# Three gaps before the tile pools of an MLP: the place of the added weight tiles modulo 256 bytes

## The chip, the cores and the metric

The kernel runs on one core of one Trainium2 chip. The metric is the device time of one execution in microseconds (us), the median of several runs. The core has five engines that run side by side, each with its own stream of instructions: TensorE (PE in the profile; PEld is its loading of weights), VectorE (DVE), ScalarE (ACT), GpSimd (POOL) and SyncE (SP, which here only issues transfers). They work on an on-chip memory of 128 partitions; a tile is a stretch of bytes at the same address in every partition. "Place modulo 256" below means that byte address modulo 256.

## The reference

One layer of an encoder, in float32, for 256 tokens of width 2048: a mixer with four groups of channels (gated linear attention, a Fourier transform, two long convolutions with learned filters, a short convolution), a cross attention to 256 memory rows, and an MLP, each with an RMS norm before it and a residual sum behind it. The change concerns the MLP alone:

```python
def swiglu(h, w_gate_up, w_down):
    gate, up = jnp.split(h @ w_gate_up, 2, axis=-1)
    return (jax.nn.silu(gate) * up) @ w_down
...
x = x + swiglu(rms_norm(x, norm_g[l, 2]), w_gate_up[l], w_down[l])
```

`w_gate_up` is 2048 x 11264 and `w_down` is 5632 x 2048.

## The kernel before

All weights come as a stream of slabs. A slab (`raw`, 128 x 2048 float32, 1 MB) holds 16 blocks of 128 x 128, in the order in which TensorE uses them. SyncE issues the transfers (`Stream.raw`, line 102) into the three buffers of pool `rawp`; during the gate/up product every fourth slab goes into one more buffer, `rawx`.

Products are made in float32r, with each float32 number split into a high and a low part: `Stream.split` casts a half slab of 1024 columns into `wh` on ScalarE (line 120) and subtracts this from the original into `wl` on VectorE (line 121). A product then takes three matmuls (`Block.part`, lines 449, 450 and 451): high by high, high by low, low by high. In the MLP the activations are the stationary operand and 512 columns of `wh` or `wl` are the moving one.

The pairs of tiles `wh` and `wl` come from pools: `wp` has three pairs, for the whole kernel; `wp2` has two more, for the gate/up product alone. `Stream.free` gives a half slab to the first of the two pools that has a pair free. A tile has 1088 columns, of which 1024 are used, starting at column `at`:

```python
at = 48 if any(a <= n < b for a, b in ROWS) else 8
...
wh, wl = (pool.tile([P, 1088], F32R, name=t, tag=t) for t in ("wh", "wl"))
wh, wl = wh[:, at:at + 1024], wl[:, at:at + 1024]
```

In the MLP `at` is 48, which is 192 bytes. The tiles of `wp` begin at 192 modulo 256, so the operand begins at 128. The tiles of `wp2` begin at 128, so there the operand begins at 64.

The MLP (`mlp`, line 853) opens pool `fp`, then `wp2`, `rawx`, `sw` (sums of activations, split) and `gp` (`u`, `m`, `g`, `h`), and calls `gate_up`; when this is done it closes them and opens `hp`, with the `held` tiles and the later `f` tiles, and calls `down`. Pools are laid out one behind the other, so a tile that is put into one pool moves all that are opened after it. `gap` (line 295) allocates such a tile and does nothing with it. The tiles with activations (`act`, `f`, the formed sums) begin at 128.

`gate_up` runs over 11 groups of 512 gate and 512 up columns, and in each over 8 pairs of 128-row steps of the contraction. Some of the pairs (two in groups 1 to 3, three in groups 4 to 10) are computed with seven products of halves in place of eight; for these VectorE also forms differences and sums of weight blocks in place in the slab (line 150). `combine` and `finish` then add the parts, apply silu and the product, turn the result (line 478) and send it to memory through GpSimd's queue (`hidden`, line 481); `fetch` brings it back (line 879). `down` (line 1025) runs over 4 groups of 512 output columns with 44 steps each; the operands of its last half slabs are the `held` tiles.

The order of the instructions is written out by the program; small pieces of other work (`Background`) are put between the matmuls at fixed points, by a count of work and not by measured time.

Of the kernel before, what the change touches and what calls it, by code (L numbers as in the profile page):

```python
# [246 lines left out]
class Block:  # L247
# [605 lines left out]
    def mlp(self):  # L853
        tc, nc, act, st = self.tc, self.nc, self.act, self.st
        with tc.tile_pool(name="fp", bufs=1) as fp:
            self.gap(fp, 192)
            f = act[4:12] + [fp.tile([P, 512], F32R, name=f"f{i}") for i in range(EARLY - 8)]
            with tc.tile_pool(name="wp2", bufs=2) as wp2, tc.tile_pool(name="rawx", bufs=1) as st.rawx, \
                    tc.tile_pool(name="sw", bufs=1) as sw, tc.tile_pool(name="gp", bufs=1) as gp:
                st.pools.append([wp2, 2])  # L860
                self.gate_up(sw, gp, f)
            st.pools.pop()
            st.rawx = None
            with tc.tile_pool(name="hp", bufs=1) as hp:
                held = [hp.tile([P, 512], F32R, name=f"held{i}") for i in range(HELD // 2)]
                self.st.places = list(zip(held[0::2], held[1::2]))
                f += [hp.tile([P, 512], F32R, name=f"g{i}") for i in range(FT - 16 - EARLY)] + self.h3
                self.bg.add(self.fetch(f, EARLY, FT, 6, SOON))
                self.down(f)
# [806 lines left out]
```

## Time and profile before

| | |
|---|---|
| median of 3 runs | 1472.63 us (1472.04 to 1472.85) |
| the profiled execution | 1474.72 us |
| its span, from the first instruction to the last | 1472.9 us |
| TensorE busy | 1458.6 us (99%) |
| VectorE busy | 1105.7 us (75%) |
| ScalarE busy | 815.1 us (55%) |
| bytes read from memory | 291.18 MB |
| mean granted clock of TensorE | 0.996 |

The page of a profile gives the busy time of each engine, its share in 40 slices of the span, the clock that TensorE was granted, and the chain of work that ended last. Views of the trace give more: windows (the busy time of each engine and the count of its instructions in a stretch of time), the timeline (instructions in order of time, with start and duration), and waits (who waited for whom). Times in views are from the start of the span. A matmul's duration in the trace is longer than the distance to the next one, because matmuls are pipelined and their ends are modelled; the distance between starts tells the pace.

### The profile page before, as it was taken

To read this page: it belongs to the slowest core of one execution; us is meant where nothing else is said; L and a number is where in the kernel's file an instruction comes from. 1 tells how busy PE (TensorE), PEld (TensorE's weight loads), DVE (VectorE), ACT (ScalarE), POOL (GpSimd) and SP (SyncE) were. 2 spreads that over 40 slices of the span, in tenths; PEclk is the share of its full clock that TensorE was granted. 3 is DMA by queue.
4 is the path that set the end of the run, shared out by engine and by line. 5 is a ranking of instruction groups with operands and counts; after the bars stand their busy time and mean duration, and the time that the engine had idled before them with its cause. 6 is when DMAs were issued, how large, how long until landed. Compare 5 with 4: busy or idle time off the path is not lost.

```text
span 1472.9 us, 19616 instructions
## 1 busy us (share of the span) xinstructions
PE 1458.6 (99%) x7275; PEld 1229.1 (83%) x7275; DVE 1105.7 (75%) x1608; ACT 815.1 (55%) x1209; POOL 161.7 (11%) x276
## 2 busy tenths in 40 slices
PE   9999999999999999999999999999999999999997
PEld 8878888898898888888888888888888888888886
DVE  6588768778767767877786888999999996644445
ACT  6556655467555546765564555555555554534344
POOL 0220100000000001100015322221101113000000
PEclk9999999999999999999999999999999999999999
DMA  9985554454535556544556865666666655655554
GB/s 351 350 262 201 204 200 172 146 182 160 208 129 204 184 180 223 180 172 174 200 203 211 273 235 205 217 218 224 223 218 241 217 196 187 243 185 192 198 198 145
DMA packets 56720, 306.11 MB, mean 208 GB/s; under 512 B 9485, under 2 KB 11182, under 8 KB 25008
## 3 DMA queue, kind: packets, MB, share of 16 engines
q1 hardware_dynamic: 45920, 281.11, 53.9%
q0 software_dynamic: 10272, 23.09, 5.3%
q8 instruction: 57, 0.93, 0.3%
q10 hardware_dynamic: 432, 0.66, 0.1%
q14 instruction: 39, 0.32, 0.1%
HBM read 291.18 MB, written 13.63 MB: 207 GB/s over the span
## 4 chain that ended last, share of the span: by engine, by line
PE 97%; DVE 1%; ACT 1%; DMA 0%; issue 0%; SPq 0%; ACTq 0%
PE pg L398 18%; PE pg L450 15%; PE pg L451 15%; PE pg L449 15%; PE pg L399 10%; PE pm L450 6%; PE pm L451 6%; PE pm L449 6%; PE pm L1177 1%; PE pg L395 1%; PE pg L396 1%; PE pm L846 1%; PE pm L819 0%; DVE wl L121 0%; DMA raw<-in_W 0%; PE pm L1557 0%
## 5 line engine op out<-in xcount | busy, mean ns | idle before, releaser
L121 DVE TENSOR_TENSOR wl<-raw,wh 128x1024 fp32r<-128x1024 f32 (+2 forms) x557 | 657.2, 1190 | 283.5 <-ACT wh L120 277.0
L120 ACT CAST wh<-raw 128x1024 fp32r<-128x1024 f32 (+2 forms) x557 | 566.3, 1023 | 521.8 <-PE pg L451 230.7
L398 PE MATMUL pg<-act,wh 128*128 128x512 f32 x1104 | 390.3, 395 | 2.9 <-DVE act L276 2.9
L399 PE MATMUL pg<-act,wl 128*128 128x256 f32 x1216 | 341.8, 281 | 0.0
L450 PE MATMUL pg<-wl,act 128*128 128x512 f32 (+1 forms) x779 | 304.1, 390 | 1.8 <-DVE wl L121 1.8
L449 PE MATMUL pg<-wh,act 128*128 128x512 f32 (+1 forms) x779 | 304.5, 392 | 0.0
L451 PE MATMUL pg<-wh,act 128*128 128x512 f32 (+1 forms) x779 | 303.9, 390 | 0.0
L398 PEld LDWEIGHTS pg<-act,wh 128*128 128x128 f32 x1104 | 208.7, 189 | 48.7 <-DVE act L276 3.3
L399 PEld LDWEIGHTS pg<-act,wl 128*128 128x128 f32 x1216 | 229.8, 189 | 0.8 <-DVE wl L121 0.5
L450 PEld LDWEIGHTS pg<-wl,act 128*128 128x128 f32 x779 | 146.4, 188 | 33.8 <-DVE wl L121 2.7
L449 PEld LDWEIGHTS pg<-wh,act 128*128 128x128 f32 x779 | 146.5, 188 | 32.5 <-issue 0.8
L451 PEld LDWEIGHTS pg<-wh,act 128*128 128x128 f32 x779 | 146.4, 188 | 31.8 <-issue 0.4
L450 PE MATMUL pm<-wl,act 128*128 128x512 f32 x288 | 112.7, 391 | 0.0
L449 PE MATMUL pm<-wh,act 128*128 128x512 f32 x288 | 112.6, 391 | 0.0
L451 PE MATMUL pm<-wh,act 128*128 128x512 f32 x288 | 112.6, 391 | 0.0
L481 POOL DMA_DIRECT2D hidden<-u x88 | 56.8, 654 | 306.0 <-DVE u L478 303.9
L150 DVE TENSOR_TENSOR raw<-raw 128x512 f32<-128x512 f32 (+1 forms) x81 | 70.2, 867 | 2.1
L449 PEld LDWEIGHTS pm<-wh,act 128*128 128x128 f32 x288 | 54.0, 187 | 12.2
L450 PEld LDWEIGHTS pm<-wl,act 128*128 128x128 f32 x288 | 54.0, 187 | 12.0
L451 PEld LDWEIGHTS pm<-wh,act 128*128 128x128 f32 x288 | 54.0, 187 | 12.0
L1014 POOL DMA_DIRECT2D xrows<-tmp x48 | 27.7, 585 | 137.6 <-DVE rc L280 126.6
L276 DVE TENSOR_TENSOR tmp<-pg,tmp 128x256 f32<-128x256 f32 x78 | 32.4, 417 | 5.4 <-ACT tmp L405 4.6
(343 smaller groups left out, 1652.0 us busy)
## 6 DMA issues: line engine op xcount, KB each, us to landing
raw<-in_W SPq DMA_DIRECT2D x246, 1024.0 KB, 5.0
raw<-in_W SPq DMA_DIRECT2D x11, 512.0 KB, 7.3
hidden<-u POOLq DMA_DIRECT2D x88, 64.0 KB, 4.7
tmp<-hidden POOLq DMA_DIRECT2D x44, 128.0 KB, 4.8
res<-in_xT SPq DMA_DIRECT2D x8, 512.0 KB, 8.3
k<-in_mem SPq DMA_DIRECT2D x8, 256.0 KB, 6.7
k<-in_x SPq DMA_DIRECT2D x8, 256.0 KB, 8.3
keys<-k POOLq DMA_DIRECT2D x32, 64.0 KB, 5.0
```

The costliest lines, as they stand in the source:

```text
L120: nc.scalar.copy(wh[:, a:b], r[:, a:b])
L121: nc.vector.tensor_tensor(out=wl[:, a:b], in0=r[:, a:b], in1=wh[:, a:b].bitcast(F32), op=ALU.subtract)
L150: op = lambda out, a, b, what=ALU.subtract: nc.vector.tensor_tensor(out=out, in0=a, in1=b, op=what)
L276: self.nc.vector.tensor_tensor(out=out, in0=a, in1=b, op=op)
L395: self.nc.tensor.matmul(p[:, 0:R], wh, slot[:, 0:R], start=start, stop=False)
L398: self.nc.tensor.matmul(p[:, :], wh, slot[:, :], start=start, stop=False)
L399: self.nc.tensor.matmul(p[:, 0:R], wl, slot[:, 0:R], start=False, stop=stop)
L449: self.nc.tensor.matmul(p, hi, wh, start=start, stop=False)
L450: self.nc.tensor.matmul(p, hi, wl, start=False, stop=False)
L451: self.nc.tensor.matmul(p, lo, wh, start=False, stop=stop)
L481: nc.gpsimd.dma_start(to[:, :, 32 * a:32 * a + 32], u[32 * a:32 * a + 32, :].rearrange("f (b t) -> f b t", t=32))
L1014: nc.gpsimd.dma_start(to[:, :, c:c + 32], u[32 * a:32 * a + 32, :].rearrange("t (b f) -> t b f", f=32))
```

## The change

Three gaps are added in `mlp`.

```diff
             self.gap(fp, 192)
             f = act[4:12] + [fp.tile([P, 512], F32R, name=f"f{i}") for i in range(EARLY - 8)]
+            self.gap(fp, 64)
             with tc.tile_pool(name="wp2", bufs=2) as wp2, tc.tile_pool(name="rawx", bufs=1) as st.rawx, \
                     tc.tile_pool(name="sw", bufs=1) as sw, tc.tile_pool(name="gp", bufs=1) as gp:
+                self.gap(sw, 192)
                 st.pools.append([wp2, 2])
                 self.gate_up(sw, gp, f)
             st.pools.pop()
             st.rawx = None
             with tc.tile_pool(name="hp", bufs=1) as hp:
+                self.gap(hp, 192)
                 held = [hp.tile([P, 512], F32R, name=f"held{i}") for i in range(HELD // 2)]
```

The first one moves `wp2` and `rawx` up by 64 bytes: the tiles of `wp2` and the buffer `rawx` go from 128 to 192 modulo 256. The second and the third one make the shift 256 bytes for what lies behind them (`sw` and `gp` in the gate/up product, `held` and the later `f` tiles in the down product), whose place modulo 256 stays. No instruction is added, removed or put elsewhere.

## Prediction

> **What bounds the kernel now.** I read the page first, for the engine that fills the span and for the granted clock.
>
> ```profile
> span 1472.9 us, 19616 instructions
> PE 1458.6 (99%) x7275; PEld 1229.1 (83%) x7275; DVE 1105.7 (75%) x1608; ACT 815.1 (55%) x1209; POOL 161.7 (11%) x276
> ...
> PEclk9999999999999999999999999999999999999999
> ...
> PE 97%; DVE 1%; ACT 1%; DMA 0%; issue 0%; SPq 0%; ACTq 0%
> ```
>
> TensorE is busy 99% of the span and is 97% of the chain that ended last, at full clock. A time that is saved between two matmuls is therefore saved at the end, as long as nothing else becomes late. So the question is only how far apart the matmuls start in the stage that the change touches, the gate/up product, and whether that distance can be set by where their operand lies.
>
> Busy time does not tell this (a matmul's row shows 0.39 us, and they overlap). I take windows from the start of one matmul to the start of a later one. A window's count is one more than the matmuls that start in it, because the one before still runs. The first table has the gate/up product and the down product.
>
> ```profile
> core 0: us, PE busy (x) PEld busy (x) DVE busy (x) ACT busy (x) POOL busy (x), PEclk, DMA share, GB/s
> ...
> 765.68:1224.52 458.84, 458.84 (x1998) 374.25 (x1997) 405.34 (x478) 250.04 (x281) 97.77 (x161) 1.00 0.65 224
> 1225.62:1456.61 230.99, 230.99 (x1020) 191.25 (x1019) 123.66 (x139) 102.14 (x130) 14.38 (x25) 1.00 0.57 199
> ```
>
> (The first matmuls of the gate/up product, before 765.68, are left out; they read pool wp.) In the down product 1019 matmuls take 230.99 us: 226.68 ns each. In the gate/up product 1997 matmuls of the same shape (128x128 stationary, 512 moving columns, float32r) take 458.84 us: 229.76 ns each. TensorE is never idle in either and the clock is 1.00 in both, so the gate/up product spends 1997 x 226.68 = 452.68 us at the down product's pace and **6.2 us on something else**. That is the whole prize, whatever causes it.
>
> To see which matmuls lose it, I followed the half slabs in the order of the program, with the address that each tile has. Moving operands in the three pairs of pool wp start at 192 + 4 x 48 bytes, that is at 128 modulo 256; those in the two pairs of wp2 start at 128 + 192, that is at 64. The next rows are the starts at which wp2 blocks begin and end (900.40 to 906.00 is two half slabs of wp2, then come three of wp), and the same stretches as windows.
>
> ```profile
> 900.40 0.39 PE L449 MATMUL pm<-wh,act 128*128 128x512 f32 x1
> ...
> 906.00 0.39 PE L449 MATMUL pm<-wh,act 128*128 128x512 f32 x1
> ...
> 908.74 0.39 PE L449 MATMUL pm<-wh,act 128*128 128x512 f32 x1
> ...
> 914.18 0.39 PE L449 MATMUL pg<-wh,act 128*128 128x512 f32 x1
> ```
>
> ```profile
> core 0: us, PE busy (x), PEclk, DMA share, GB/s
> 900.40:906.00 5.60, 5.60 (x25) 1.00 1.01 381
> 906.00:908.74 2.74, 2.74 (x13) 1.00 0.70 295
> 908.74:914.18 5.44, 5.44 (x25) 1.00 0.34 104
> 972.08:977.68 5.60, 5.60 (x25) 1.00 0.00 0
> 1001.82:1008.64 6.82, 6.82 (x31) 1.00 0.94 358
> 1451.17:1456.61 5.44, 5.44 (x25) 1.00 0.00 0
> ```
>
> From wp2, 24 matmuls take 5.60 us: 233.3 ns each. From wp, 24 take 5.44 us: 226.7 ns each. The difference, 6.67 ns, does not come from transfers: the wp2 window at 972 has a DMA share of 0.00 and the same 5.60 us, and the wp window at 1001.82 has a share of 0.94 and takes 6.82 us for 30 matmuls (227.3 ns). Nor does it come from the region of memory: the window at 1451 reads its moving operand from the held tiles, which lie at bytes 168,064 and up, where wp2 lay before, but start at 128 modulo 256, and its 24 matmuls take 5.44 us. The first window after a wp2 block is a little slow (2.74 us for 12, where 12 x 226.7 = 2.72): about 20 ns of catching up follow each block.
>
> **The change, part by part.** Instructions, their order and their waits stay the same on every engine and queue; only start addresses move. So there is nothing to add or remove, and each step is a change of duration.
>
> Gap of 64 bytes in fp. It moves wp2 and rawx up by 64 bytes. The moving operands in wp2 then start at 192 + 192 = 384, that is 128 modulo 256, like those in wp. Of the 1997 matmuls 792 take their moving operand from wp2 (two of the five pairs, so about two fifths; counted by the tiles' addresses). 792 x 6.67 ns = 5.28 us. The catching up goes too: there are 46 changes from wp2 back to wp, 46 x 20 ns = 0.92 us. Sum 6.2 us, which is the 6.2 us that the stage loses as a whole, worked out above without the addresses. All of it lies on the path, as TensorE has no idle time there.
>
> The buffer rawx moves from 128 to 192 modulo 256, where the three of rawp already are. No row groups transfers by address, so I bound it: the rows of waits below name no wait of TensorE, and none of ScalarE for a landing of raw, in the whole stage. Below, nothing: a transfer that lands earlier feeds no one earlier. Above, nothing until it eats the time by which the operands are ahead. I take zero.
>
> ```profile
> ACT wh L120 <- PE pg L451: 78.3, 64, 2.2
> ACT wh L120 <- PE pm L451: 68.6, 57, 2.2
> ACT wh L120 <- DVE raw L150: 41.9, 28, 2.4
> DVE wl L121 <- ACT wh L120: 41.5, 45, 1.8
> ```
>
> These rows (total us, times, longest) are of the stage from 766 to 1224 us. ScalarE's casts into wh wait 146.9 us for TensorE to give a tile back, so the makers of operands are ahead and held up by the reader.
>
> Gaps of 192 bytes in sw and hp. With the 64 they make 256, so the formed sums, u, m, g, h, the held tiles and the later f tiles keep their place modulo 256. Price zero both ways, by the held window (5.44 us) that already has this place.
>
> The casts and subtractions. They write wl and wh at 128 in wp and at 64 in wp2 today. VectorE does not fill the stage (405.34 of 458.84 us), so a change of some ns in either is hidden; the cover is that idle 53.5 us. But it is thinner in places, and a faster TensorE eats into it. The tightest operand that I found is the second half slab of the group that starts at 981.1 us:
>
> ```profile
> 980.49 1.18 DVE L121 TENSOR_TENSOR wl<-raw,wh 128x1024 fp32r<-128x1024 f32 x1
> ...
> 982.74 0.39 PE L450 MATMUL pm<-wl,act 128*128 128x512 f32 x1
> ...
> 1140.00:1160.00 20.00, 20.00 (x89) 16.40 (x88) 19.63 (x24) 11.33 (x13) 5.14 (x8) 1.00 0.51 155
> ```
>
> It is ready at 981.67 and used at 982.74, 1.07 us ahead. Near 1150 VectorE is busy 19.63 of 20 us, so in such a stretch it cannot follow a faster TensorE. But in each group of columns (11 groups in 459 us, some 42 us each) it also reaches the point where it waits for tiles, so what TensorE gains adds up over one group at most: 6.2 / 11 = 0.56 us. That is less than 1.07. The next thing to be late is this add, with 0.5 us left.
>
> By the sum the profiled execution, 1474.72 us with a span of 1472.9, would take 1468.5. The median of the three runs is 2.1 us below the profiled one; from it, 1472.63 - 6.2 = **1466.4 us**, 0.42% less.
>
> The Trainium skill, page "SBUF — State Buffer", section "Specifications (TRN2)", gives memory lines of 16 bytes and full bandwidth where each line is hit at least twice. Both 64 and 128 are multiples of 16 and the operand is contiguous, so by that page alone the start would not matter and the time would stay 1472.6. The windows above do not agree that nothing else matters (233.3 against 226.7 ns).
>
> **The rivals.**
> No change: what sets 233.3 ns is not the start modulo 256 but something else that goes with wp2, such as the order in which its tiles are used. For it: the rows cannot vary one without the other inside the pool. Against it: the held window, in the same region, and four different places of wp2 with one pace. Time 1472.6. The page named above would give the same.
>
> Gain given back: the adds become late and TensorE waits. For it: 19.63 of 20 us. Against: 0.56 us against 1.07. If each group lost half of its gain, 3.1 us would remain: 1469.5.
>
> Slower: all five pairs then share one place modulo 256, and a tile that is being written collides with the one that is read, so that all 1997 matmuls run at 233.3 ns. It decides if the quick pace of wp needs that its neighbours lie elsewhere. Price: 1997 x 6.67 = 13.3 us in place of 6.2, so 1472.6 + 7.1 = 1479.7. Against it: in the down product only the three wp pairs are in use, all at one place, written and read at once, at 226.68 ns.
>
> **How the numbers follow.** The forecast gets 0.88, no change 0.05, the gain half given back 0.04, slower 0.03. The runs of before spread over 0.8 us, and without the catching up the gain is 5.3 us (1467.3); so 1465.4 to 1468.2 holds about 8 in 10. No more than 6.2 us can be had, as none of the windows has a pace under 226.7 ns; the lower end is noise alone. 0.2% is 2.9 us, about what a measurement can tell from no change. Faster by more: the forecast and most of the half gain, 0.91; within: 0.06; slower: 0.03.
>
> **What the changed profile would show.** The window from the first to the last matmul of the gate/up product should fall from 458.84 to 452.7 us for the same count; two half slabs of wp2 should take 5.44 us. The down product's 230.99 us for 1019 should stay. Against the forecast would be a window that stays at 5.60 us for wp2, a wp window above 5.44, or idle time of TensorE before L450 with VectorE's L121 as what ended it. A granted clock under 1.00 in the stage would make it wrong in another way.

## The result, and the profile after

The changed kernel takes 1467.55 us (median of 6 runs, 1465.87 to 1469.45) against 1473.21 us before (median of 6, 1472.04 to 1477.14). The ratio is 0.9958 with a 95% interval of 0.9948 to 0.9968, so 4.7 to 7.7 us less; by the ratio itself 6.2 us, while the two medians differ by 5.7. The page of the changed kernel has nearly the same shares as that of before:

```profile
span 1467.7 us, 19616 instructions
PE 1452.5 (99%) x7275; PEld 1229.2 (84%) x7275; DVE 1105.3 (75%) x1608; ACT 814.5 (55%) x1209; POOL 161.4 (11%) x276
...
PE 97%; DVE 1%; ACT 1%; DMA 0%; issue 0%; SPq 0%; ACTq 0%
```

TensorE is still what bounds the kernel, VectorE and ScalarE work as long as before, and only PE's busy time fell, by 6.1 us. The windows from the start of the first undisturbed matmul of the gate/up product to its end, and over the down product up to its last matmul, say where (columns as in the prediction):

```profile
core 0: us, PE busy (x) PEld busy (x) DVE busy (x) ACT busy (x) POOL busy (x), PEclk, DMA share, GB/s
766.59:1219.26 452.67, 452.67 (x1998) 374.89 (x1997) 404.97 (x478) 249.42 (x281) 97.65 (x161) 1.00 0.66 227
1220.36:1459.08 238.72, 238.72 (x1054) 197.70 (x1053) 125.50 (x145) 105.73 (x136) 14.35 (x25) 1.00 0.57 197
```

The gate/up product takes 452.67 us for the 1997 matmuls that took 458.84, so 226.67 ns each. The down product has 1053 in 238.72 us, 226.70 ns, as before. Three windows show that nothing is left to tell the pools apart; the first and the last are two half slabs of wp2 (24 matmuls), the middle one three of wp (36), which follow a wp2 block:

```profile
core 0: us, PE busy (x), PEclk, DMA share, GB/s
836.42:841.86 5.44, 5.44 (x26) 1.00 0.99 384
841.86:850.02 8.16, 8.16 (x38) 1.00 0.27 111
794.26:799.70 5.44, 5.44 (x26) 1.00 0.98 328
```

(Where a window's edge is rounded down, one more matmul is counted, 26 in place of 25.) wp2 went from 5.60 to 5.44 us, and after it 36 matmuls of wp take 8.16 us, 226.7 ns each: the catching up is gone.

The profiled execution's span fell by 5.2 us and not by 6.2, as its gate/up product begins 0.9 us later than in the execution of before (766.59 against 765.68). That lies ahead of everything that the change touches, and it is spread: in the profiles below that leave the stage before as it is, the same point lies between 762.7 and 766.3 us. The MLP itself hardly varies: its gate/up product takes 452.66 or 452.67 us here, in wp2_only and in both64.

### The profile page after: what moved, and what is told of

It is laid out like the page before. It is cut to its first block, busy times and chain, and to the rows that moved or that the text cites. A ratio compares the mean times of both kernels' runs of the same rounds, so it can differ in the third digit from the quotient of the medians.

```text
span 1467.7 us, 19616 instructions
## 1 busy us (share of the span) xinstructions
PE 1452.5 (99%) x7275; PEld 1229.2 (84%) x7275; DVE 1105.3 (75%) x1608; ACT 814.5 (55%) x1209; POOL 161.4 (11%) x276
## 4 chain that ended last, share of the span: by engine, by line
PE 97%; DVE 1%; ACT 1%; DMA 0%; issue 0%; SPq 0%; ACTq 0%
PE pg L398 18%; PE pg L450 15%; PE pg L451 15%; PE pg L449 15%; PE pg L399 10%; PE pm L449 6%; PE pm L451 6%; PE pm L450 6%; PE pm L1180 1%; PE pg L395 1%; PE pg L396 1%; PE pm L846 1%; PE pm L819 1%; DVE wl L121 0%; DMA raw<-in_W 0%; PE pm L1560 0%
```

## The experiments

All medians below are beside runs of the kernel before on the same chip. Its median there was 1473.83 to 1474.16 us where an interval is given, so kernels are compared by their ratios: 0.9958 is the changed kernel.

**Which of the two moved pools it is.** The first kernel moves wp2 alone, the second rawx alone; what lies behind keeps its place.

```diff
 wp2_only: the first gap stays (fp, 64), and the second one goes into rawx
-                self.gap(sw, 192)
+                self.gap(st.rawx, 192)
```

```diff
 rawx_only
-            self.gap(fp, 64)
...
+                self.gap(st.rawx, 64)
                 self.gap(sw, 192)
...
-                self.gap(hp, 192)
+                self.gap(hp, 256)
```

> Only the wp2 tiles move (128 to 192 modulo 256); rawx stays at 128, everything behind keeps its place. Place theory (the start of the moving operand modulo 256 sets the pace): as the full change, 6.2 us under before, the gate/up stretch near 452.7 us, two half slabs of wp2 in 5.44 us. Rival (the place of rawx does it): as before, 458.8 us and 5.60 us.

> Only the buffer rawx moves (128 to 192 modulo 256); wp2 stays at 128, so its operands start at 64. Place theory: no change from before within 0.8 us, two half slabs of wp2 in 5.60 us. Rival (the place of rawx does it): 6.2 us under before.

wp2_only: 1467.61 us, ratio 0.996 (0.9946 to 0.9974). rawx_only: 1474.16 us, ratio 1.0001 (0.9992 to 1.001). The gate/up product in both, first of wp2_only:

```profile
764.91:1217.57 452.66, 452.66 (x1998) 374.76 (x1997) 404.83 (x478) 249.88 (x281) 97.89 (x161) 1.00 0.65 227
```

and of rawx_only, with its first two half slabs of wp2:

```profile
764.93:1223.77 458.84, 458.84 (x1999) 374.26 (x1997) 405.50 (x478) 250.28 (x281) 97.90 (x161) 1.00 0.64 224
...
765.39:770.99 5.60, 5.60 (x25) 1.00 0.93 316
```

The whole gain belongs to wp2. Whether the buffer rawx begins at 128 or at 192 makes no difference to the time.

**All five pairs at 64.** If 64 is what is slow, then wp must become slow as well.

```diff
-        at = 48 if any(a <= n < b for a, b in ROWS) else 8
+        at = 32 if n >= GU else 48 if any(a <= n < b for a, b in ROWS) else 8
```

> The changed kernel with the start column 32 in place of 48 in the whole MLP, so every moving operand of wp and wp2 starts at 64 modulo 256. Place theory: all matmuls that read them at 233.3 ns, in the gate/up product 2031 and in the down product 1008 (48 of 1056 read held tiles): 3039 x 6.67 ns = 20.3 us above the changed kernel, near 1487.8, 14 us above before. Rival one (wp2 is slow by something else that the change removed): as the changed kernel, 1467.5. Rival two (the slow pace came of places that differ between neighbours): again 226.7 ns, 1467.5.

Measured: 1488.27 us, ratio 1.0099 (1.0084 to 1.0114), 20.8 us above the changed kernel by the ratios. The gate/up and the down product:

```profile
766.03:1231.99 465.96, 465.96 (x1998) 375.39 (x1997) 406.62 (x478) 250.73 (x281) 97.89 (x161) 1.00 0.64 220
1233.10:1478.54 245.44, 245.44 (x1055) 196.95 (x1053) 125.43 (x145) 105.89 (x136) 14.39 (x25) 1.00 0.55 191
```

The gate/up product has 233.3 ns in every matmul (465.96 / 1997), in wp as in wp2. Both rivals fall: the pool and its order play no part, and neither does whether neighbours lie at the same place.

**The first gap without the two others.** This leaves wp2 as in the change and moves the formed sums, the held and the later f tiles to 192.

```diff
-                self.gap(sw, 192)
...
-                self.gap(hp, 192)
```

> The first gap alone, without the two gaps of 192: wp2 as in the change, but the formed sums, u, m, g, h, the held tiles and the later f tiles go to 192 modulo 256. Place of the moving operand alone: at most the 48 matmuls that read held tiles change, 0.3 us, so 1467.5 within the spread. If the place of the stationary operand counts as much: 324 matmuls with formed sums and 288 with the later f tiles at up to 6.67 ns, 4.1 us, so up to 1471.6.

Measured: 1473.25 us, ratio 0.9993 (0.9984 to 1.0003): nearly all of the gain is lost. Gate/up and down:

```profile
762.67:1218.22 455.55, 455.55 (x1998) 374.85 (x1997) 405.13 (x478) 250.34 (x281) 97.90 (x161) 1.00 0.66 225
...
1219.32:1459.90 240.58, 240.58 (x1053) 197.49 (x1052) 125.49 (x145) 106.10 (x136) 14.41 (x25) 1.00 0.56 195
```

The gate/up product loses 2.9 us and the down product some 2.1 (228.7 ns for each of 1052). The 324 matmuls with formed sums and the 288 with later f tiles read their moving operand at 128, the quick place. By their starts they are 233.8 and 233.3 ns apart, as the stationary operand now begins at 192. These matmuls alone make up about the 4.1 us that were expected; the rest of the 5.0 is the catching up behind them and the held tiles. So **the start of the moving operand alone does not set the pace**; the stationary one counts too. The prediction's rule needed another form.

**Eight places of the stationary operand.** One run:

```diff
-            f = act[4:12] + [fp.tile([P, 512], F32R, name=f"f{i}") for i in range(EARLY - 8)]
+            f = act[4:12]
+            for i in range(EARLY - 8):
+                f.append(fp.tile([P, 512], F32R, name=f"f{i}"))
+                self.gap(fp, 32)
```

> The changed kernel with a gap of 32 bytes behind each of the eight f tiles, so that as stationary operands of the down product they begin at 128, 160, 192, 224, 0, 32, 64 and 96 modulo 256; the moving operands stay at 128. Moving operand alone: 226.7 ns with each of the eight. If the stationary operand counts as the moving one does: 6.67 ns more with the one at 64, over 24 matmuls. The total changes by less than 1.3 us (192 x 6.67 ns) either way.

The six matmuls with each f tile in the first column group, with the tile's place 128, 160, 192, 224, 0, 32, 64 and 96 in this order:

```profile
1229.22:1230.58 1.36, 1.36 (x7) 1.00 0.48 75
1230.58:1231.97 1.39, 1.39 (x7) 1.00 0.80 306
1231.97:1233.37 1.40, 1.40 (x7) 1.00 0.89 375
1233.37:1234.77 1.40, 1.40 (x7) 1.00 0.00 0
1234.77:1236.17 1.40, 1.40 (x8) 1.00 0.59 88
1236.17:1237.57 1.40, 1.40 (x7) 1.00 0.82 328
1237.57:1238.95 1.38, 1.38 (x7) 1.00 0.82 344
1238.95:1240.36 1.41, 1.41 (x8) 1.00 0.69 180
```

Only the tile at 128 has 1.36 us (6 x 226.7); the seven others have 1.38 to 1.41. The total is 1468.81 us. By the starts the down product is 1.2 us longer than in the changed kernel, under the 1.3 us that were expected as the most.

**Both at 64.** If what counts is whether the two operands begin at the same place, then 64 must be as good as 128 once both are there. A gap ahead of all tiles moves everything by 192:

```diff
+        self.gap(cp, 192)
         self.act = [cp.tile([P, 512], F32R, name=f"act{i}") for i in range(24)]
```

> The changed kernel with a gap of 192 bytes ahead of all tiles, so that everything moves by 192: in the MLP the moving and the stationary operands start at 64 modulo 256, each where the slow wp2 operands started. Relation theory (the pace is 226.7 ns when the moving and the stationary operand start at the same place modulo 256, and slower otherwise): as the changed kernel, 1467.5, gate/up near 452.7 us. Place theory of the prediction (the start of the moving operand alone; 64 is slow): 233.3 ns for all 3087 MLP matmuls, 20.6 us more, 1488.

Measured: 1467.51 us, ratio 0.9958 (0.9941 to 0.9975).

```profile
764.59:1217.26 452.67, 452.67 (x1998) 374.76 (x1997) 404.96 (x478) 249.40 (x281) 97.63 (x161) 1.00 0.65 227
1218.36:1456.90 238.54, 238.54 (x1054) 197.55 (x1053) 125.50 (x145) 105.69 (x136) 14.35 (x25) 1.00 0.56 197
```

The same 452.67 us as the changed kernel, with every moving operand at the place that was slow in wp2. That is what the theory of the relation expects, and the prediction's rule is refuted.

**Moving at 128, stationary at 64.** The same kernel with `at` 0 in the MLP:

```diff
+        self.gap(cp, 192)
         self.act = [cp.tile([P, 512], F32R, name=f"act{i}") for i in range(24)]
...
-        at = 48 if any(a <= n < b for a, b in ROWS) else 8
+        at = 0 if n >= GU else 48 if any(a <= n < b for a, b in ROWS) else 8
```

> The same with the start column 0 in the MLP, so that the moving operands in wp and wp2 start at 128 and the stationary ones at 64 modulo 256. Relation theory: 233.3 ns for the 3039 matmuls that read wp and wp2, 20.3 us above the changed kernel, 1487.8. Place theory of the prediction (moving operand at 128 is quick): as the changed kernel, 1467.5.

Measured: 1474.25 us, ratio 1.0003 (0.9994 to 1.0012): slower than the changed kernel by 6.6 us, so neither expectation. The direction is that of the relation theory, the size a third of it:

```profile
764.76:1221.86 457.10, 457.10 (x1999) 374.99 (x1997) 405.40 (x478) 250.18 (x281) 97.61 (x161) 1.00 0.65 224
```

457.10 / 1997 is 228.9 ns. I had taken every unequal pair to cost 6.67 ns; a moving operand that starts 64 bytes above the stationary one costs 2.2, while one that starts 64 bytes below it (wp2 before, and fp_only) costs 6.67 or a little more. So the difference counts with its sign.

**The start of the moving operand at every 4 bytes.** One run, with `at` counted up from half slab to half slab through the MLP; the stationary operands stay at 128.

```diff
+        if n >= GU:
+            at = self.turn % 64
+            self.turn += 1
```

> The changed kernel with the start column of each half slab in the MLP counted up from 0 to 63 and over again, so the moving operands start at every multiple of 4 bytes modulo 256. Place theory: the distance between starts is a function of the start alone, the same in wp and wp2: 226.7 ns at 128, 233.3 ns at 64, and at the others values that it does not give (by the two known ones, between 220 and 240). Rival (something else of wp2): one pace at all starts within a pool. The time by the mean of the two known values, 230.0 ns for all 3039: 10 us above the changed kernel, 1477.7.

Measured: 1488.51 us, beside 1474.77 for the kernel before on that chip (one run each). By the ratio this is 20 us above the changed kernel, where I had 10. Stretches of 12 matmuls, with the moving operand at 4 (wp2), 192 (wp2), 192 (wp), 4 (wp), 64 (wp) and 128 (wp):

```profile
1191.86:1194.73 2.87, 2.87 (x13) 1.00 0.00 0
906.01:908.76 2.75, 2.75 (x13) 1.00 1.01 413
1305.37:1308.12 2.75, 2.75 (x13) 1.00 0.70 212
1352.82:1355.69 2.87, 2.87 (x14) 1.00 0.36 151
1394.84:1397.65 2.81, 2.81 (x14) 1.00 0.71 233
1439.75:1442.48 2.73, 2.73 (x14) 1.00 0.68 219
```

The same place gives the same time in both pools. By the starts of the last six matmuls of each half slab, free of catching up, 128 has 226.7 ns and is the lowest of all 64 places. The steps of 4 bytes count too: 124 has 228.9, 132 has 238.2, 4 and 116 have 240.0. The mean over all these matmuls is 233.1 ns, well above the 230.0 in the middle of the two that I knew, which is the miss in the total.

The paces fit one table by the difference of the starts, moving minus stationary, modulo 256:

| difference | measured with (moving, stationary) | ns between starts |
|---|---|---|
| 0 | (128, 128) changed kernel; (64, 64) both64 | 226.7; 226.7 |
| 64 | (128, 64) act64; (192, 128) sweep | 228.9; 228.8 |
| 128 | (0, 128) sweep; (128, 0) frot | 233.3; 233.0 |
| 192 | (64, 128) before, all64; (128, 192) fp_only | 233.3; 233.3 and 233.8 |

Each difference was met at two places and has the same pace at both, within what the short stretches tell. The four other differences of frot (32, 96, 160 and 224) have 231.8 to 233.8 ns over 24 matmuls each, and sweep, with the stationary operand elsewhere, has the same at each within 1.5 ns.

**The products outside the MLP.** There the weights are stationary (at 224 with `at` 8) and the activations move (at 128). A rule "equal is best" would ask for `at` 48.

```diff
-        at = 48 if any(a <= n < b for a, b in ROWS) else 8
+        at = 48
```

> The changed kernel with the start column 48 everywhere, so that in the products outside the MLP where the weights are stationary they start at 128 modulo 256 in place of 224; the moving activations start at 128. Relation theory: the 1168 matmuls of 512 columns at line 398 go from 230 to 226.7 ns, 3.9 us less, near 1463.6. Rival (the relation matters only where the weights move, or the narrow matmuls at line 399 lose by it): 1467.5 or more.

Measured: 1472.79 us, ratio 0.9992 (0.9982 to 1.0001), 5.0 us above the changed kernel. From the first matmul of line 398 to the last of 399, first the changed kernel, then at48:

```profile
195.47:758.22 562.75, 559.30 (x3335) 0.99 0.52 180
```

```profile
196.42:761.76 565.34, 562.06 (x3334) 1.00 0.50 179
```

In that stage at48 is 2.6 us longer than the profiled execution of the changed kernel, and 4.0 longer than that of wp2_only, which has the same tiles there (561.37). In the ten profiles that leave this stage as it is, it takes 559.8 to 562.7 us, so at48 lies outside their spread. There a matmul of 512 columns (line 398) alternates with one of 256 (line 399). By the starts, an undisturbed pair takes 346.9 ns in the changed kernel and 350.5 in at48, over nearly 1100 pairs each. For 1168 pairs this is 4.2 us.

But in at48 the pairs do not have one pace. The next rows are two long stretches of 213 and 221 pairs, first of at48, then the same pairs in the changed kernel:

```profile
487.07:560.91 73.84, 73.84 (x428) 1.00 0.50 180
683.43:761.52 78.09, 78.09 (x444) 1.00 0.49 176
...
485.82:559.66 73.84, 73.84 (x428) 1.00 0.52 176
681.37:757.98 76.61, 76.61 (x444) 1.00 0.51 179
```

The first stretch of at48 has 346.7 ns for each pair, as the changed kernel has in both, and the second has 353.3. Both operands begin at 128 modulo 256 in both stretches. So where the widths alternate the two starts alone do not set the pace; what else does is open. The table above holds for the pattern of the MLP, three matmuls of 512 columns, and is not carried over. Two more kernels, one run each, go through eight and then all 64 places of the stationary weights:

```diff
+        at = 48
+        if not any(a <= n < b for a, b in ROWS):
+            at = self.turn % 8 * 8
+            self.turn += 1
```

(the second with `self.turn % 64`)

> The changed kernel with the start column counted through 0, 8 to 56 in the products with stationary weights, so that these start at 192, 224, 0, 32, 64, 96, 128 and 160 modulo 256 while the activations move at 128. Relation theory: line 398 is quickest (226.7 ns) at 128 and slower at the other seven. Rival: one pace, 230 ns, at all eight.

> The changed kernel with the start column counted from 0 to 63 in the products with stationary weights, so that these start at every multiple of 4 bytes modulo 256 while the activations move at 128. A pair of matmuls (512 columns at line 398, then 256 at line 399) takes 347.0 ns with the start at 224 in the changed kernel, and 346.9 to 353.6 ns at the eight starts tried. If 224 is as good as any: no start under 345 ns, and the total some us above the changed kernel. If a start between them is better: a pair under 345 ns, worth 1.17 us of the whole kernel for each ns.

In the first, an undisturbed pair between pairs of the same place took 347.0 ns at 224 and 347.1 at 96, and 349.7 to 352.6 at the six others, with some 100 pairs each. In the second it took from 346.1 (at 116) to 357.1, with 347.3 at 224, in samples of 4 to 18 pairs. The totals were 1471.51 and 1472.34 us. As at48 shows two paces at one place, such short samples do not rank the places; 224 is among the quick ones in all of them. None of these kernels is quicker than the changed one.

## Why the prediction was right

The time was 1467.55 us where 1466.4 was forecast, inside the range of 1465.4 to 1468.2. By the ratio the change is 6.2 us, as forecast. The time itself is 1.15 us above the forecast. Half of this is the start: the forecast set out from a median of 1472.63 for the kernel before, and six runs have 1473.21. The rest is within the spread of the runs.

*The prize of 6.2 us, from the windows.* Right: 458.84 to 452.67 is 6.17 us, and the down product kept its 226.7 ns.

*792 x 6.67 ns and 46 x 20 ns.* Right in both terms: wp2's two half slabs went from 5.60 to 5.44 us, and the window that follows has the plain pace.

*rawx at zero.* Right; rawx_only measured it alone (1.0001).

*The gaps in sw and hp at zero.* Right as a price, since the place stays. But here there was luck: the reason that I gave looked at the held tiles, which are moving operands, and asked nothing of the stationary ones. What these two gaps prevent is 5.0 us (fp_only), nearly as much as the whole gain.

*The cover of VectorE.* Right: the tightest operand of that kind is ready at 979.94 and used at 980.80, 0.86 us ahead where it was 1.07, so it lost 0.2 of the 0.56 us that I allowed.

```profile
978.76 1.18 DVE L121 TENSOR_TENSOR wl<-raw,wh 128x1024 fp32r<-128x1024 f32 x1
...
980.80 0.39 PE L450 MATMUL pm<-wl,act 128*128 128x512 f32 x1
```

*The rule: quick because the moving operand starts at 128.* Wrong as a rule, right in its result, because every stationary operand of the MLP begins at 128 as well. The trace of before had no MLP product with a stationary operand anywhere but at 128, so it could not tell the place of one operand from the difference between the two, and the prediction names no such rival. both64 and act64 told them apart: 64 is quick where the other is at 64 too, and 128 is slower where the other is at 64.

*The rivals.* No change is refuted by the result, and "the order in which the tiles are used" by all64. The collision of tiles at one place is refuted by the changed kernel itself, which has all of them there at 226.67 ns. The gain given back did not occur.

*The page's rule.* The Trainium skill, "SBUF — State Buffer", section "Specifications (TRN2)", has lines of 16 bytes. By these alone nothing would have changed, as the prediction says. The runs decide otherwise: moving operands that start at 128, 192 and 64, all multiples of 16, have 226.7, 228.8 and 233.3 ns, with the stationary one at 128 (sweep).

Open: why the difference matters in the chip. While a matmul streams its moving operand the next stationary one is already loaded (in the profile of before a load of 0.19 us begins at 900.41 and a matmul at 900.40), so the two reads go on at once. That they get into each other's way by their distance in memory is argued, not shown; no run took the load away.

```profile
900.41 0.19 PEld L450 LDWEIGHTS pm<-wl,act 128*128 128x128 f32 x1
```

## What to carry to other kernels

Where TensorE is the bound, divide windows between starts by the count of matmuls, one window for each buffer: equal shapes with a different pace point to where the operands lie, and the busy column does not show it. Test the stationary and the moving start together: move each alone, and then both by the same amount, as only this tells a place from a difference. When tiles are inserted, look at what lies behind them in memory: a shift of 64 bytes there would have cost 5.0 of the 6.2 us here.

## What the hardware showed that I had not expected

In the MLP, where float32r matmuls of 512 columns follow each other and each has a new stationary operand, the pace depends on the start of the moving operand minus that of the stationary one modulo 256 bytes, with its sign: 226.7 ns at 0, 228.9 at 64, 233.3 at 128 and at 192. It depends on it down to 4 bytes: 238.2 ns at 4, 228.9 at 252. After a block with a slow difference the next matmuls lose some 20 ns together before they have their own pace (2.74 us for 12 in place of 2.72). Where 512 and 256 columns alternate, this does not carry over: at equal starts a pair took 346.7 ns in one long stretch and 353.3 in another, and with the stationary operand 96 bytes above the moving one it took 346.7 in both.
